# A transposed second copy of x: the first unit of a streaming encoder loads and normalises x in the layout that its projection reads

## The chip, the cores and the metric

One core of a Trainium2 chip. The metric is the device time of one execution in microseconds. The kernel was run three times, and one further execution was profiled; times of single instructions come from that profile.

## The reference

One layer of a hybrid encoder over a prompt of 2048 frames and 32 frames of a running stream, in float32. What matters here is the head of it:

```python
def rmsnorm(x, g):
    xf = x.astype(jnp.float32)
    y = xf * lax.rsqrt(jnp.mean(xf * xf, axis=-1, keepdims=True) + EPS)
    return (y * g.astype(jnp.float32)).astype(x.dtype)
...
        h = rmsnorm(yp, norm_gain[l])
        qa, ka, va, ga, qb, kb, vb, gb = split_proj(h, w_in[l])   # h @ w_in, 1024 -> 4096
        ...
        oa = band_attention_prompt(qa, ka, va, rel_bias[l])       # 8 heads x 64, own chunk and 8 before
        ob = diff_subnorm(diff_attention_prompt(qb, kb, vb, lam), subln_gain[l], lambda_init)
        yp = yp + merge_out(oa, ga, ob, gb, w_out[l])
```

A final RMS norm follows, and the new rows of the key and value caches are outputs too.

## The kernel before

The prompt is cut into 8 chunks of 256 frames (`NCH`), the 4096 columns of the input projection into 8 units of 512: units 0 to 3 are two heads of branch A each, 4 to 7 one head of branch B. The loop over `steps` takes one unit after the other (`order`), and in each unit the 8 chunks. A step projects a chunk, splits queries, keys and values, forms the softmax rows of its attention and finishes the attention of the step before.

Every float32 operand of a product is split into a high part, rounded to float32r, and a low part, the rest; a product is three matmuls (high x high, high x low, low x high). `project` (L250) takes them with the frames as the stationary operand, `project_T` (L258) with the weights; both walk over 8 k steps of 128 model columns. They need h transposed, with model columns on the partitions: tile `hT`, two parts x 8 k x 256 frames, in two buffers.

In the first unit `make_hT` (L218) builds `hT` for each chunk. `load_x` (L193) brings two tiles of 128 frames, each as two halves of 512 columns. `norm_rows` (L199) squares them on ScalarE with a sum along the row, works out one scale per frame on VectorE and ScalarE (`rstd_of`, L179) and scales the halves in place on POOL (L209). TensorE transposes them in blocks of 128x128, four to a PSUM tile (L226); ScalarE copies out the high part (L229) and VectorE subtracts for the low part (L230). SP then writes `hT` to a scratch tensor (L231), from which the later seven units load it (`load_T`). The norm's gain is folded into the weights: `load_w` (L159) loads 8 tiles of 128x512; for the first unit POOL makes gain x weight as the high part (L173) and VectorE the low part (L174).

The order of instructions on each engine is set by a planner, from the order of the program, from priorities (`ahead(n)` moves what is in it n places forward) and from a timeline that it works out; each engine then takes its instructions strictly in that order. Loads and stores are issued by SP. Tiles with tag "e" (128x512) share 16 buffers: halves of x, weights as loaded, scratch rows. PSUM tiles with tag "t" have two buffers, used by all transposes. `subnorm` (L412), in branch B, has a sum over partitions as a matmul with `onesd`, a 128x128 tile that holds 1/128 (L416).

Of the kernel before, what the change touches and what calls it, by code (L numbers as in the profile page):

```python
# [8 lines left out]
F32 = mybir.dt.float32  # L9
F32R = mybir.dt.float32r  # L10
AF = mybir.ActivationFunctionType
ALU = mybir.AluOpType
AX = mybir.AxisListType

P = 128
D = 1024
# [3 lines left out]
KT = D // P  # L20
NT = SEQ // P
NCH = NT // 2
EPS = 1e-6
LAMBDA_INIT = 0.2
NEG = -1.0e30
BAND = 640
# [4 lines left out]
def hybrid_step(  # L31
    ctx: ExitStack,
    tc: tile.TileContext,
    x_p: bass.AP,
    x_s: bass.AP,
    cak: bass.AP,
    cav: bass.AP,
# [54 lines left out]
    def e_tile(name):  # L92
        return pool.tile([P, 512], F32, name=name, tag="e", bufs=16)
# [10 lines left out]
    def t_psum():  # L104
        return psum.tile([P, 512], F32, name="t_ps", tag="t", bufs=2)
# [34 lines left out]
    def dma_here(**kw):  # L140
        tc.keep_in_program_order(SP.dma_start(**kw))
# [14 lines left out]
        ACT.activation(le, ls, AF.Exp)  # L156
        DVE.scalar_tensor_tensor(nlam, le[:, 1:2], LAMBDA_INIT, le[:, 0:1], ALU.subtract, ALU.subtract)

    def load_w(wsrc, cur_b, gain=None, tags=(("w", 10),) * KT):  # L159
        his, los = [], []  # L160
        for k in range(KT):
            raw = pool.tile([P, BAND], F32, name="wraw", tag="ea", bufs=4)[:, 0:512] if cur_b else e_tile("wraw")
            SP.dma_start(out=raw, in_=wsrc[k])
            tag, bufs = tags[k]
            w = pool.tile([P, 2, 512], F32R, name="w", tag=tag, bufs=bufs)
            hi, lo = w[:, 0, :], w[:, 1, :]
            g = 1.0 if gain is None else gain[:, k:k + 1]
            if cur_b and gain is not None and k % 2 == 0:
                ACT.activation(hi, raw, AF.Copy, scale=g)
                POOL.tensor_scalar(raw, raw, g, 0.0, ALU.mult, ALU.add)  # L170
                POOL.tensor_tensor(lo, raw, hi.bitcast(F32), ALU.subtract)  # L171
            else:
                POOL.tensor_scalar(hi, raw, g, 0.0, ALU.mult, ALU.add)  # L173
                DVE.scalar_tensor_tensor(lo, raw, g, hi.bitcast(F32), ALU.mult, ALU.subtract)  # L174
            his.append(hi)
            los.append(lo)
        return his, los
# [15 lines left out]
    def load_x(src, rows):  # L193
        xt = row_tiles("xt")
        for j in range(2):
            SP.dma_start(out=xt[j][0:rows], in_=src[:, j * 512:(j + 1) * 512])
        return xt

    def norm_rows(xt, rows):  # L199
        junk = e_tile("junk")  # L200
        ss = st_tile("ss", 2)
        for j in range(2):
            ACT.activation(junk[0:rows], xt[j][0:rows], AF.Square, accum_out=ss[0:rows, j:j + 1])
        s1 = st_tile("ss1", 1)
        DVE.tensor_tensor(s1[0:rows], ss[0:rows, 0:1], ss[0:rows, 1:2], ALU.add)
        r = rstd_of(s1, D, rows)
        for j in range(2):
            x = xt[j][0:rows]
            POOL.tensor_scalar(x, x, r[0:rows, 0:1], 0.0, ALU.mult, ALU.add)  # L209
        return xt  # L210
# [1 line left out]
    def ht_tile():  # L212
        return pool.tile([P, 2, KT, 256], F32R, name="hT", tag="hT", bufs=2)

    def load_x_chunk(c):
        return [load_x(x_pv[t * P:(t + 1) * P, :], P) for t in (2 * c, 2 * c + 1)]

    def make_hT(c, xts):  # L218
        with ahead(250):
            hT = ht_tile()  # L220
            for tt in range(2):
                h = norm_rows(xts[tt], P)
                for g in range(2):
                    tp = t_psum()
                    for j in range(4):
                        PE.transpose(out=tp[:, j * P:(j + 1) * P], in_=h[g][:, j * P:(j + 1) * P], identity=ident)  # L226
                    tv = tp.rearrange("p (k t) -> p k t", k=4)
                    ks, ts = slice(4 * g, 4 * g + 4), slice(tt * P, (tt + 1) * P)
                    ACT.copy(out=hT[:, 0, ks, ts], in_=tv)  # L229
                    DVE.tensor_tensor(hT[:, 1, ks, ts], tv, hT[:, 0, ks, ts].bitcast(F32), ALU.subtract)  # L230
            SP.dma_start(out=hT_d[c].bitcast(F32), in_=hT.bitcast(F32))  # L231
        return hT

# [422 lines left out]
        DVE.tensor_tensor(oTs[:, u, NS:2 * NS], og[:, 0:NS], oTs[:, u, 0:NS].bitcast(F32), ALU.subtract)  # L656

    ngain = const.tile([P, KT], F32, name="ngain")
    dma_here(out=ngain, in_=norm_gain)
    order = [0, 4, 5, 1, 6, 2, 7, 3]  # L660
    pend = None
    pend_s = None
# [6 lines left out]

    steps = [(n, c) for n in range(len(order)) for c in range(NCH)]  # L670

    xts = {0: load_x_chunk(0)}

    def get_hT(i):
        if i >= len(steps):
# [5 lines left out]
        return load_T(hT_d[c])  # L681

    hTn = get_hT(0)
    xts[1] = load_x_chunk(1)
    Ws = {0: load_w(w_in[order[0] // 4, order[0] % 4], False, ngain)}
    for i, (n, c) in enumerate(steps):
        u = order[n]
        isB = u >= 4
# [10 lines left out]
        QH, QL = next(qkv)  # L699
        gate = None  # L700
        if n == 0 and c + 2 < NCH:
            xts[c + 2] = load_x_chunk(c + 2)
        hTn = get_hT(i + 1)
        if n == 0 and c == 1:
            small_loads()
# [29 lines left out]
    for t in range(NT + 1):  # L735
# [31 lines left out]
            SP.dma_start(out=dst[:, cs], in_=y)  # L767


_INS = ['x_prompt', 'x_sample', 'cache_a_k', 'cache_a_v', 'cache_b_k', 'cache_b_v', 'norm_gain', 'w_in', 'w_out',  # L770
        'bias_p', 'bias_s', 'lams', 'subln', 'final_gain', 'rope_c', 'rope_s']
_OUTS = [((1, 2048, 1024), 'float32'), ((1, 32, 1024), 'float32'),
# [6 lines left out]
def _layout(inputs):  # L779
    import numpy as np  # L780
    a = {k: np.asarray(v) for k, v in inputs.items()}
    w = a['w_in'][0].reshape(KT, P, 2, 4, 4, P)
    r = {k: a[k] for k in ('x_prompt', 'x_sample', 'cache_a_k', 'cache_a_v', 'cache_b_k', 'cache_b_v', 'norm_gain')}
    r['w_in'] = w.transpose(2, 4, 0, 1, 3, 5).reshape(2, 4, KT, P, 512)
    r['w_out'] = a['w_out'][0].reshape(KT, P, 2, 512).transpose(2, 0, 1, 3)
    rb = a['rel_bias'][0]
# [40 lines left out]
```

## Time and profile before

| | us |
|---|---|
| runs | 1626.01, 1623.29, 1625.41 |
| median | 1625.41 |
| span of the profiled execution, first to last instruction | 1624.3 |
| TensorE busy in it | 1568.4 |
| VectorE busy | 1110.5 |
| ScalarE busy | 997.0 |
| POOL busy | 654.6 |

The profile gives no time of its own for the profiled execution beside its span; the span lies inside the range of the runs and 1.1 us below their median. In the rows below L12 is line 12 of the kernel. PE is TensorE's matmul, DVE is VectorE, ACT ScalarE, POOL GpSimd, SP the engine that issues the DMAs. A matmul's duration runs until its result is out, so successive matmuls overlap: what one costs is read from the distance between starts.

### The profile page before, as it was taken

To read this page: it belongs to the slowest core of one execution; us is meant where nothing else is said; L and a number is where in the kernel's file an instruction comes from. 1 tells how busy PE (TensorE), PEld (TensorE's weight loads), DVE (VectorE), ACT (ScalarE), POOL (GpSimd) and SP (SyncE) were. 2 spreads that over 40 slices of the span, in tenths; PEclk is the share of its full clock that TensorE was granted. 3 is DMA by queue.
4 is the path that set the end of the run, shared out by engine and by line. 5 is a ranking of instruction groups with operands and counts; after the bars stand their busy time and mean duration, and the time that the engine had idled before them with its cause. 6 is when DMAs were issued, how large, how long until landed. Compare 5 with 4: busy or idle time off the path is not lost.

```text
span 1624.3 us, 30799 instructions
## 1 busy us (share of the span) xinstructions
PE 1568.4 (97%) x10612; PEld 1453.1 (89%) x10612; DVE 1110.5 (68%) x3048; ACT 997.0 (61%) x2717; POOL 654.6 (40%) x1129
## 2 busy tenths in 40 slices
PE   7999999989999899999999999999999999989997
PEld 6899999978998799999998899999998999978885
DVE  5776757897588866675788856676789677743333
ACT  5776557777577766656777766565777666531111
POOL 5453434465145544353345544353446444520000
PEclk9999999999999999999999999999999999999999
DMA  7643453333332224335432153344423263334562
GB/s 275 225 172 119 176 208 131 131 122 130 125 137 86 97 102 178 122 128 195 162 136 79 66 186 124 131 148 167 159 89 129 84 240 131 131 132 161 172 210 67
DMA packets 92972, 233.92 MB, mean 144 GB/s; under 512 B 9776, under 2 KB 51888, under 8 KB 75376
## 3 DMA queue, kind: packets, MB, share of 16 engines
q1 hardware_dynamic: 92816, 231.96, 40.0%
q8 instruction: 84, 1.38, 0.3%
q14 instruction: 72, 0.59, 0.1%
HBM read 179.10 MB, written 53.74 MB: 143 GB/s over the span
## 4 chain that ended last, share of the span: by engine, by line
PE 77%; DVE 11%; ACT 5%; issue 3%; POOL 2%; DMA 1%; SPq 0%; DVEq 0%; POOLq 0%; ACTq 0%
PE z_ps L254 11%; PE z_ps L255 11%; PE z_ps L256 11%; PE t_ps L387 6%; PE z_ps L261 5%; PE z_ps L263 5%; PE z_ps L262 5%; PE s_ps L379 4%; PE s_ps L378 4%; DVE nmx L466 2%; PE o_ps L556 2%; PE o_ps L555 2%; DVE e L479 2%; DVE w L174 2%; PE o_ps L501 1%
## 5 line engine op out<-in xcount | busy, mean ns | idle before, releaser
L255 PE MATMUL z_ps<-w,hT 128*128 128x256 f32 (+2 forms) x1280 | 424.1, 332 | 4.1 <-POOL w L171 2.4
L254 PE MATMUL z_ps<-w,hT 128*128 128x256 f32 (+2 forms) x1280 | 424.7, 332 | 2.5 <-ACT hT L229 1.2
L256 PE MATMUL z_ps<-w,hT 128*128 128x256 f32 (+2 forms) x1280 | 424.1, 331 | 0.0
L255 PEld LDWEIGHTS z_ps<-w,hT 128*128 128x128 f32 x1280 | 243.5, 190 | 22.4 <-POOL w L171 3.4
L254 PEld LDWEIGHTS z_ps<-w,hT 128*128 128x128 f32 x1280 | 243.7, 190 | 19.3 <-ACT hT L229 1.7
L468 ACT ACTIVATE e<-s_ps,nmx 128x512 f32<-128x512 f32 (+3 forms) x320 | 199.1, 624 | 98.6 <-DVE nmx L466 90.5
L256 PEld LDWEIGHTS z_ps<-w,hT 128*128 128x128 f32 x1280 | 243.7, 190 | 14.1 <-issue 0.5
L397 DVE TENSOR_TENSOR pl<-t_ps,ph 128x512 fp32r<-128x512 f32 (+1 forms) x312 | 192.6, 623 | 77.8 <-ACT ph L396 75.4
L261 PE MATMUL z_ps<-hT,w 128*128 128x256 f32 x768 | 220.3, 287 | 1.7 <-DVE ql L344 1.7
L263 PE MATMUL z_ps<-hT,w 128*128 128x256 f32 x768 | 218.9, 285 | 0.0
L396 ACT CAST ph<-t_ps 128x512 fp32r<-128x512 f32 (+1 forms) x312 | 163.0, 535 | 90.5 <-PE o_ps L555 42.4
L262 PE MATMUL z_ps<-hT,w 128*128 128x256 f32 x768 | 218.4, 284 | 0.0
L378 PE MATMUL s_ps<-ks,qh 128*128 128x512 f32 (+2 forms) x544 | 194.0, 366 | 10.5 <-ACT e L468 7.8
L466 DVE TENSOR_REDUCE nmx<-s_ps 128x1 f32<-128x512 f32 (+3 forms) x320 | 187.9, 600 | 13.1 <-PE s_ps L379 9.8
L379 PE MATMUL s_ps<-ks,ql 128*128 128x512 f32 (+2 forms) x544 | 187.7, 357 | 0.1
L474 POOL TENSOR_SCALAR e<-e,da 128x512 f32<-128x512 f32 (+3 forms) x160 | 110.3, 704 | 168.5 <-DVE da L444 132.8
L261 PEld LDWEIGHTS z_ps<-hT,w 128*128 128x128 f32 x768 | 145.5, 190 | 4.9 <-PE o_ps L416 1.2
L262 PEld LDWEIGHTS z_ps<-hT,w 128*128 128x128 f32 x768 | 145.4, 189 | 2.1 <-issue 0.5
L263 PEld LDWEIGHTS z_ps<-hT,w 128*128 128x128 f32 x768 | 145.4, 189 | 1.6 <-issue 0.5
L533 POOL TENSOR_SCALAR ea<-ea,sma 128x640 f32<-128x640 f32 (+4 forms) x128 | 96.3, 754 | 115.3 <-DVE sma L532 98.7
L531 ACT ACTIVATE ea<-ea,nma 128x640 f32<-128x640 f32 (+4 forms) x128 | 97.3, 760 | 62.6 <-DVE nma L529 61.4
L378 PEld LDWEIGHTS s_ps<-ks,qh 128*128 128x128 f32 x544 | 102.2, 190 | 19.3 <-ACT e L468 12.0
(192 smaller groups left out, 3422.3 us busy)
## 6 DMA issues: line engine op xcount, KB each, us to landing
hT<-hTd SPq DMA_DIRECT2D x112, 1024.0 KB, 7.0
wraw<-in_w_in_dram SPq DMA_DIRECT2D x64, 256.0 KB, 5.0
hTd<-hT SPq DMA_DIRECT2D x8, 2048.0 KB, 7.3
oTd<-oT SPq DMA_DIRECT2D x64, 256.0 KB, 3.2
hT<-oTd SPq DMA_DIRECT2D x16, 1024.0 KB, 6.1
out_dram<-z SPq DMA_DIRECT2D x160, 64.0 KB, 1.6
xt<-in_x_prompt_dram SPq DMA_DIRECT2D x32, 256.0 KB, 5.4
y<-in_x_prompt_dram SPq DMA_DIRECT2D x32, 256.0 KB, 6.5
```

The lines of the kernel that those rows point to most:

```text
L254: PE.matmul(zp, hT[:, 0, k, ts], his[k][:, cols], start=(k == 0), stop=False)
L255: PE.matmul(zp, hT[:, 0, k, ts], los[k][:, cols], start=False, stop=False)
L256: PE.matmul(zp, hT[:, 1, k, ts], his[k][:, cols], start=False, stop=(k == KT - 1))
L261: PE.matmul(zp, his[k][:, cols], hT[:, 0, k, :], start=(k == 0), stop=False)
L262: PE.matmul(zp, his[k][:, cols], hT[:, 1, k, :], start=False, stop=False)
L263: PE.matmul(zp, los[k][:, cols], hT[:, 0, k, :], start=False, stop=(k == KT - 1))
L378: PE.matmul(sp[:, 0:w], QH[:, m, qs], ks[:, m, kc], start=True, stop=False)
L379: PE.matmul(sp[:, 0:w], QL[:, m, qs], ks[:, m, kc], start=False, stop=True)
L396: ACT.copy(out=hv, in_=tv)
L397: DVE.tensor_tensor(lv, tv, hv.bitcast(F32), ALU.subtract)
L466: DVE.tensor_reduce(nmx[:, m, b:b + 1], sp[:, 0:w], AX.X, ALU.max, negate=True)
L468: ACT.activation(e[:, 0:w], sp[:, 0:w], AF.Exp, bias=nmx[:, m, b:b + 1], accum_out=sm[:, m, b:b + 1])
```

## The change

The host lays x out a second time, `x_t`, as chunk x 128 partitions x 8 k x 256 frames. `load_xT` loads a chunk of it as four tiles of 128 x (2 k x 256 frames), 256 KB each as before. `scales_T` squares them on ScalarE, adds the four tiles and the two k of the rest to one 128x256 tile (VectorE for the first chunk, POOL for the others), and sums it over the partitions with one matmul with `onesd`, which leaves the sum on all partitions; the scale per frame is then worked out as a whole 128x256 tile `rb`. `make_hT` multiplies each tile by `rb` on VectorE, copies the high part on ScalarE and subtracts for the low part on POOL. There are no transposes of the prompt's x left on TensorE. The 32 frames of the running stream are treated as before, and the last stage still reads x row by row.

The weights of the first unit are loaded ahead of the second chunk's x, four of the eight tiles in buffers of another tag ("ea"); their high parts are made on ScalarE and POOL in turn, their low parts on VectorE. The load of the gain, the first chunk's loads and these weights get priorities further forward.

```diff
-    def load_w(wsrc, cur_b, gain=None, tags=(("w", 10),) * KT):
+    def raw_w(wsrc, k, ea):
+        raw = pool.tile([P, BAND], F32, name="wraw", tag="ea", bufs=4)[:, 0:512] if ea else e_tile("wraw")
+        SP.dma_start(out=raw, in_=wsrc[k])
+        return raw
+
+    def load_w(wsrc, cur_b, gain=None, tags=(("w", 10),) * KT, raws=None):
...
+            if raws is not None:
+                if k % 2:
+                    ACT.activation(hi, raw, AF.Copy, scale=g)
+                else:
+                    POOL.tensor_scalar(hi, raw, g, 0.0, ALU.mult, ALU.add)
+                DVE.scalar_tensor_tensor(lo, raw, g, hi.bitcast(F32), ALU.mult, ALU.subtract)
+            elif cur_b and gain is not None and k % 2 == 0:
...
-    def load_x_chunk(c):
-        return [load_x(x_pv[t * P:(t + 1) * P, :], P) for t in (2 * c, 2 * c + 1)]
-
-    def make_hT(c, xts):
+    def load_xT(c, js=range(4)):
+        xs = [e_tile("xT").rearrange("p (k t) -> p k t", k=2) for _ in js]
+        for x, j in zip(xs, js):
+            SP.dma_start(out=x, in_=x_t[c, :, 2 * j:2 * j + 2, :])
+        return xs
+
+    def scales_T(xs, add):
+        sq = [e_tile("sqT").rearrange("p (k t) -> p k t", k=2) for _ in xs]
+        for a, x in zip(sq, xs):
+            ACT.activation(a, x, AF.Square)
+        add(sq[0], sq[0], sq[1], ALU.add)
+        add(sq[2], sq[2], sq[3], ALU.add)
+        add(sq[0], sq[0], sq[2], ALU.add)
+        sm = sq[0][:, 0, :]
+        add(sm, sm, sq[0][:, 1, :], ALU.add)
+        ps = t_psum()[:, 0:256]
+        PE.matmul(ps, onesd, sm, start=True, stop=True)
+        v = pool.tile([P, 256], F32, name="vT", tag="sq", bufs=1)
+        DVE.tensor_scalar(v, ps, P / D, EPS, ALU.mult, ALU.add)
+        r = pool.tile([P, 256], F32, name="rT", tag="rs", bufs=1)
+        ACT.activation(r, v, AF.Ln)
+        ACT.activation(r, r, AF.Exp, scale=-0.5)
+        rb = pool.tile([P, 256], F32, name="rb", tag="rb", bufs=1)
+        DVE.tensor_tensor(rb, r, r, ALU.mult)
+        DVE.tensor_tensor(rb, rb, v, ALU.mult)
+        DVE.tensor_scalar(rb, rb, -0.5, 1.5, ALU.mult, ALU.add)
+        DVE.tensor_tensor(rb, rb, r, ALU.mult)
+        return rb
+
+    def make_hT(c, xs):
         with ahead(250):
             hT = ht_tile()
-            for tt in range(2):
-                h = norm_rows(xts[tt], P)
-                for g in range(2):
-                    tp = t_psum()
-                    for j in range(4):
-                        PE.transpose(out=tp[:, j * P:(j + 1) * P], in_=h[g][:, j * P:(j + 1) * P], identity=ident)
-                    tv = tp.rearrange("p (k t) -> p k t", k=4)
-                    ks, ts = slice(4 * g, 4 * g + 4), slice(tt * P, (tt + 1) * P)
-                    ACT.copy(out=hT[:, 0, ks, ts], in_=tv)
-                    DVE.tensor_tensor(hT[:, 1, ks, ts], tv, hT[:, 0, ks, ts].bitcast(F32), ALU.subtract)
+            rb = scales_T(xs, DVE.tensor_tensor if c == 0 else POOL.tensor_tensor)
+            for j, x in enumerate(xs):
+                ks = slice(2 * j, 2 * j + 2)
+                DVE.tensor_tensor(x, x, rb.unsqueeze(1).broadcast_to([P, 2, 256]), ALU.mult)
+                ACT.copy(out=hT[:, 0, ks, :], in_=x)
+                POOL.tensor_tensor(hT[:, 1, ks, :], x, hT[:, 0, ks, :].bitcast(F32), ALU.subtract)
             SP.dma_start(out=hT_d[c].bitcast(F32), in_=hT.bitcast(F32))
         return hT
...
-    dma_here(out=ngain, in_=norm_gain)
+    with ahead(1100):
+        SP.dma_start(out=ngain, in_=norm_gain)
...
-    xts = {0: load_x_chunk(0)}
+    wsrc = w_in[order[0] // 4, order[0] % 4]
+    with ahead(1000):
+        xts = {0: load_xT(0)}
+        raws = [raw_w(wsrc, k, k < 4) for k in range(KT)]
...
     hTn = get_hT(0)
-    xts[1] = load_x_chunk(1)
-    Ws = {0: load_w(w_in[order[0] // 4, order[0] % 4], False, ngain)}
+    with ahead(200):
+        Ws = {0: load_w(wsrc, True, ngain, raws=raws)}
+    xts[1] = load_xT(1)
...
-            xts[c + 2] = load_x_chunk(c + 2)
+            xts[c + 2] = load_xT(c + 2)
...
+    r['x_t'] = a['x_prompt'][0].reshape(NCH, 256, KT, P).transpose(0, 3, 2, 1)
```

## Rows read from the trace of the kernel before

**Rows 1.** The page: busy time of each engine, and its chain by engine.

```profile
PE 1568.4 (97%) x10612; PEld 1453.1 (89%) x10612; DVE 1110.5 (68%) x3048; ACT 997.0 (61%) x2717; POOL 654.6 (40%) x1129
...
PE 77%; DVE 11%; ACT 5%; issue 3%; POOL 2%; DMA 1%; SPq 0%; DVEq 0%; POOLq 0%; ACTq 0%
```

**Rows 2.** Stretches, chunks 1-4: us, busy PE PEld DVE ACT POOL, clock, DMA, GB/s.

```profile
30.30:45.40 15.10, 15.10 (x128) 15.02 (x127) 8.03 (x29) 9.28 (x27) 2.93 (x7) 1.00 0.33 140
45.40:64.80 19.40, 16.90 (x135) 15.93 (x133) 13.00 (x51) 16.55 (x53) 7.00 (x12) 1.00 0.78 279
64.80:85.00 20.20, 19.89 (x154) 19.63 (x155) 16.70 (x53) 15.06 (x43) 10.56 (x21) 0.92 0.50 184
85.00:108.60 23.60, 22.13 (x177) 21.02 (x177) 19.92 (x68) 19.47 (x61) 15.58 (x29) 1.00 0.43 151
```

**Rows 3.** Timeline of TensorE at a group of transposes: start, us, instruction, count.

```profile
80.87 0.28 PE L262 MATMUL z_ps<-hT,w 128*128 128x256 f32 x1
80.99 0.60 PE L226 MATMUL t_ps<-ident,xt 128*128 128x128 f32 x4
81.34 0.36 PE L556 MATMUL o_ps<-pl,vt 128*128 128x256 f32 x1
81.55 0.28 PE L555 MATMUL o_ps<-ph,vt 128*128 128x256 f32 x1
```

**Rows 4.** Timeline of TensorE at a column sum (L416) of the second unit.

```profile
245.31 0.59 PE L416 MATMUL o_ps<-sq,onesd 128*128 128x256 f32 x2
245.55 0.47 PE L261 MATMUL z_ps<-hT,w 128*128 128x256 f32 x1
245.85 0.28 PE L262 MATMUL z_ps<-hT,w 128*128 128x256 f32 x1
```

**Rows 5.** Timeline of TensorE ahead of chunk 3; idle before, releaser in brackets.

```profile
62.61 1.33 PE L226 MATMUL t_ps<-ident,xt 128*128 128x128 f32 x8 [1.66 <-POOL xt L209]
...
64.76 0.39 PE L254 MATMUL z_ps<-w,hT 128*128 128x256 f32 x1 [0.83 <-ACT hT L229]
```

**Rows 6.** Groups by shape, POOL: count | busy us, mean ns | idle before.

```profile
L477 POOL TENSOR_TENSOR e<-e 128x512 f32<-128x512 f32 x40 | 58.1, 1454 | 0.3
...
L171 POOL TENSOR_TENSOR w<-wraw,w 128x512 fp32r<-128x512 f32 x16 | 22.3, 1402 | 0.1
L209 POOL TENSOR_SCALAR xt<-xt,rr 128x512 f32<-128x512 f32 x32 | 21.9, 697 | 11.7 <-ACT rr L185 5.9 <-DVE rr L190 2.4 <-DMA xt<-in_x_prompt_dram 2.3
```

**Rows 7.** The same of VectorE, then one of ScalarE.

```profile
L479 DVE SCALAR_TENSOR_TENSOR e<-e,da 128x512 f32<-128x512 f32 x72 | 74.1, 1034 | 14.6 <-POOL e L474 14.3
...
L766 DVE SCALAR_TENSOR_TENSOR y<-y,rr,fg 128x512 f32<-128x512 f32 x32 | 23.0, 760 | 0.6
...
L230 DVE TENSOR_TENSOR hT<-t_ps,hT 128x512 fp32r<-128x512 f32 x32 | 21.7, 687 | 9.5 <-ACT hT L229 9.3
...
L421 DVE SCALAR_TENSOR_TENSOR on<-o_ps,gcol,rs 128x256 f32<-128x256 f32 x32 | 15.1, 471 | 5.2 <-ACT rs L419 5.1
...
L419 ACT ACTIVATE rs<-rs 128x256 f32<-128x256 f32 x32 | 13.4, 418 | 0.4
```

**Rows 8.** By stretch, POOL's row scalings (L209) alone, chunks 2 to 4.

```profile
45.40:64.80 19.40, 2.29 (x4) 1.00 0.78 279
64.80:85.00 20.20, 5.99 (x9) 0.92 0.50 184
85.00:108.60 23.60, 6.80 (x10) 1.00 0.43 151
```

**Rows 9.** Timeline of the start: ScalarE, TensorE, VectorE, and POOL last.

```profile
7.52 0.63 ACT L203 ACTIVATE junk<-xt 128x512 f32<-128x512 f32 x1 [0.46 <-DMA xt<-in_x_prompt_dram]
...
13.27 0.56 PE L254 MATMUL z_ps<-w,hT 128*128 128x256 f32 x1
...
20.68 0.74 DVE L174 SCALAR_TENSOR_TENSOR w<-wraw,ngain,w 128x512 fp32r<-128x512 f32 x1
...
12.04 8.11 POOL L173 TENSOR_SCALAR w<-wraw,ngain 128x512 fp32r<-128x512 f32 x8 [0.17 <-DMA wraw<-in_w_in_dram]
```

More of the change, by code (lines that the diff above doesn't have):

```diff
@@ L34, in hybrid_step @@
     x_p: bass.AP,
+    x_t: bass.AP,
     x_s: bass.AP,
@@ L157, in small_loads @@
         DVE.scalar_tensor_tensor(nlam, le[:, 1:2], LAMBDA_INIT, le[:, 0:1], ALU.subtract, ALU.subtract)
-    def load_w(wsrc, cur_b, gain=None, tags=(("w", 10),) * KT):
+    def raw_w(wsrc, k, ea):
[3 more added lines that the diff above has]
+    def load_w(wsrc, cur_b, gain=None, tags=(("w", 10),) * KT, raws=None):
         his, los = [], []
         for k in range(KT):
-            raw = pool.tile([P, BAND], F32, name="wraw", tag="ea", bufs=4)[:, 0:512] if cur_b else e_tile("wraw")
-            SP.dma_start(out=raw, in_=wsrc[k])
+            raw = raw_w(wsrc, k, cur_b) if raws is None else raws[k]
             tag, bufs = tags[k]
@@ L167, in load_w @@
             g = 1.0 if gain is None else gain[:, k:k + 1]
-            if cur_b and gain is not None and k % 2 == 0:
+            if raws is not None:
[5 more added lines that the diff above has]
+            elif cur_b and gain is not None and k % 2 == 0:
                 ACT.activation(hi, raw, AF.Copy, scale=g)
@@ L767, in hybrid_step @@
             SP.dma_start(out=dst[:, cs], in_=y)
-_INS = ['x_prompt', 'x_sample', 'cache_a_k', 'cache_a_v', 'cache_b_k', 'cache_b_v', 'norm_gain', 'w_in', 'w_out',
+_INS = ['x_prompt', 'x_t', 'x_sample', 'cache_a_k', 'cache_a_v', 'cache_b_k', 'cache_b_v', 'norm_gain', 'w_in', 'w_out',
         'bias_p', 'bias_s', 'lams', 'subln', 'final_gain', 'rope_c', 'rope_s']
```

## The prediction

> **What bounds the kernel now.** I read the page's busy times first, then the chain that ended last: TensorE is busy for 97% of the span and carries 77% of the chain [rows 1]. The reader is to see there that time comes off this kernel only where TensorE gets less to do or waits less. The change works in the first unit alone, so I cut that unit into its chunks with busy times by stretch (each stretch starts with the first projection matmul of a chunk): in chunks 1 to 4 TensorE is busy for all but a little, and POOL for 3 to 16 of the 15 to 24 us [rows 2]. Then the timeline of TensorE, for what a transpose and a float32 column sum cost between other matmuls [rows 3, 4] and where TensorE stands idle [rows 5]. Last the groups of instructions, for the price of what the other engines gain and lose [rows 6, 7], and the start [rows 9].
>
> **TensorE.** *Removed:* 16 transposes a chunk, in groups of four. One group starts at 80.99, and the next matmul at 81.34; that matmul is followed after 0.21 us, where the one ahead of the group was followed after 0.12 [rows 3]. So a group costs 0.35 + 0.09 = 0.44 us of TensorE and a chunk 4 x 0.44 = 1.76 us. *Added:* one column sum a chunk, a float32 product of onesd with 256 columns. The trace has it elsewhere: L416 writes the same shape, as two instructions. It starts at 245.31, the second matmul after it at 245.85; less the 0.12 us of the one between, it costs 0.54 - 0.12 = 0.42 us [rows 4]. Net 1.76 - 0.42 = 1.34 us a chunk, and over chunks 1 to 7, where TensorE is full, 7 x 1.34 = **9.4 us** less. Chunk 0 is in the start, below.
>
> **The one stall of TensorE in this unit.** Ahead of chunk 3 TensorE waits 1.66 us for POOL's normalised rows and 0.83 us for ScalarE's copy [rows 5], and in the stretch after it the granted clock is 0.92 on average, that is 1.2 GHz for a part of it and 2.4 GHz for the rest; 20.2 us x 0.08 = 1.6 us of work lost [rows 2]. The waited-for instructions (row scale, transposes, copy out of PSUM) all go. What is late next is the column sum and the low parts, costed below as pacing; the old stall itself I count as gone: 2.5 + 1.6 = **4.1 us** less. Its bounds are 0 (the new chain stalls at the same place) and 4.1.
>
> **POOL, and what it can take back.** *Removed:* four row scalings of 0.70 us a chunk [rows 6]. *Added*, from chunk 1 on: three sums of 128x512 and one of 128x256, and the four low parts of 128x512, all two-input operations out of SBUF. The same form is there twice: 1.45 us (L477) and 1.40 us (L171) [rows 6]. Seven at 1.43 and one at half of that make 10.7 us a chunk in place of 2.8. Beside it stands POOL's other work, the stretch's busy time less the row scalings: 2.9 at most in chunk 1, 7.0 - 2.3 = 4.7 in chunk 2, 10.6 - 6.0 = 4.6 in chunk 3, 15.6 - 6.8 = 8.8 in chunk 4 [rows 2, 8]. So POOL comes to 13.6, 15.4, 15.3 and 19.5 us, while TensorE, less the 1.34 us and the stall, would need 15.1 - 1.3 = 13.8, 19.4 - 2.5 - 1.3 = 15.6, 20.2 - 1.6 - 1.3 = 17.3 and 23.6 - 1.3 = 22.3 us. In chunks 1 and 2 the two engines are even; in chunk 3 there are 2 us of room, in chunk 4 nearly 3. The row scalings were done ahead in bunches (nine and more in the stretches of chunks 3 and 4 [rows 8], four to a chunk); the new sums can go ahead as well, but the low parts can't: they wait for one of the two hT buffers. TensorE's projection takes one low part for two of its eight k steps, so a POOL that comes late holds the projection there. For the three builds that fall into the start and chunks 1 and 2 I take 1.5 us each, **4.5 us** more, about one two-input operation late per build. The bounds are 0 and the full path: sums 5.0 + low parts 5.7 = 10.7 us against the 2.8 of today, nearly 8 us a build.
>
> The trace shows VectorE's form with two SBUF inputs at 1.03 us where POOL is busy and at 0.76 where it is idle, so a busy POOL costs it 0.27 us an operation [rows 7]. The Trainium skill ("SBUF — State Buffer", Who interferes with whom) goes further: the port pair that VectorE and GPSIMD share is an exclusive lock, so a VectorE operation with two SBUF inputs and a GPSIMD operation that reads SBUF would never run together. By the rows I have the pacing above; by that rule it would be the first rival below.
>
> **VectorE and ScalarE.** *VectorE:* four low parts of 0.69 us out of PSUM go [rows 7], with ten one-column operations that I leave out on the safe side. In come four products of 128x512 with rb, both inputs in SBUF: the bounds for that form are 0.76 us with POOL idle (L766) and 1.03 us with POOL busy (L479), and I take the upper one since POOL will be busy [rows 7]; and five of 128x256 at no more than 0.47 (L421) [rows 7]. That is 4.1 + 2.4 - 2.8 = 3.7 us a chunk more, on an engine busy for 8.0 of 15.1 and 19.9 of 23.6 us in the stretches [rows 2]; it stays just under TensorE, so it costs nothing by itself, but if its cover goes in chunk 4 (19.9 + 3.7 = 23.6 against 22.3 us for TensorE) it costs 1.3 us. *ScalarE:* squares and copies stay four each; a logarithm and an exponential of 0.42 us [rows 7] come in for reads of accumulators and one-column functions: even.
>
> **The chain of one build** is longer. From the last square today: statistics, row scale, transposes, copy: the last square of chunk 0 starts at 7.52 and the first projection matmul runs at 13.3. New: sums, column sum, five operations and two functions of 0.42 to 0.47, product, copy. VectorE makes the sums in chunk 0, and of them only two follow the last square (0.8 and 0.5 us), so 8.2 + 1.3 + 0.9 (the column sum at half clock) + 7 x 0.45 + 1.0 + 0.6 = about 15.1: 1.8 us later. **Start:** against that, W's eight loads go ahead of the second chunk's x. Today POOL makes eight high parts from 12.04 to 20.15 and VectorE's last low part ends at 21.42 [rows 9], which paces TensorE. Then four high parts go to ScalarE, and POOL is free for them. VectorE has 8 low parts, 3.5 sums and 4 products at 0.9, the middle of L766 and L479, and 2.4 us of scales [rows 7]: 16.4 us. From the last square's start without a pause it ends at 23.9, less what it did before, against 21.4. I take **0** for the start: the earlier W against the later x; bounds -1.5 and +2.5. The queue of SP: the norm gain stays first, x of chunk 0 next, W past x of chunk 1 (four issues); the second chunk is due at 30, more than 10 us behind its landing either way.
>
> **The sum.** -9.4 - 4.1 + 4.5 + 0 = -9.0 us. The profiled execution's span is 1624.3 us; the median of the runs is 1625.4, 1.1 us above it, which I take as it is. 1624.3 - 9.0 + 1.1 = **1616.4 us**. With the bounds of the terms short of the full pacing the forecast's own range is 1610 to 1622. All later units are as full of TensorE as this one [rows 1], so what comes off here has no other engine to be given back to; but the order of later instructions is planned anew, and I allow 2 us to either side for that.
>
> **Rivals.** *VectorE and POOL get in each other's way, no change.* If the two couldn't read SBUF at the same time at all, the chunk would need their sum: for chunks 1 to 3 13.6, 15.4 and 15.3 on POOL plus 4 x 0.76 + 3 x 0.47 = 4.4 on VectorE, 18.0, 19.8 and 19.7 us against 13.8, 15.6 and 17.3: 4.2 + 4.2 + 2.4 = 10.8 us back, and with some 2 us in chunk 4 12.8 of the gain of 9.4 + 4.1 = 13.5 is gone: 1624.7. Against it: at the start POOL's eight and VectorE's eight weight operations, 8 x 0.70 (POOL's one-input price at L209) + 8 x 0.76 = 11.7 us alone, are done between 12.04 and 21.42, in 9.4 us [rows 6, 7, 9]: they overlap in part. So the trace shows slowing, but no full exclusion.
>
> *The column sum stands in TensorE's queue, slower.* TensorE takes its instructions in order. The column sum waits for POOL's last sum; behind it in the queue stand the attention matmuls of the chunk before and then the projection. If POOL makes the 5.0 us of sums behind its softmax scalings instead of ahead, TensorE stands for them in each of seven builds. It decides once a build loses more than the 1.34 us that it gains. At half of the sums exposed, 2.5 us a build, and 1.3 us of lost clock with it (today's one stall of 2.5 us cost 1.6), it is 7 x 3.8 = 26.6 us more against 13.5 less: 1638.5. For it: POOL goes to 99% of TensorE's time in chunks 1 and 2, and its queue has waits of its own. Against: 16 buffers of this size let x and its squares be loaded and summed a chunk ahead.
>
> **Chances.** Forecast (1610 to 1622): 0.55. No change: 0.2, some of it still just faster. Slower by the column sum: 0.25. A measurement of this kernel tells 0.2%, 3.3 us, from no change. Faster 0.58, same 0.17, slower 0.25. The range 1607 to 1635 takes in the forecast, the case without change and the lower half of the slower one.
>
> **What would show it.** Right: no transposes at the old place and groups of two column-sum instructions instead; TensorE without a wait in chunks 1 to 3, projection matmuls at their 0.12 us pitch; the first matmul of the second unit about 9 us earlier. Wrong: waits of the column sum for POOL, or of the third projection matmul of a k step for the low part; POOL over 95% busy in chunks 1 to 4; a granted clock below 0.95 in those stretches; VectorE's products with rb well above 1.03 us; a start that ends more than 2 us later.

## The result, and the profile after

| | before | after |
|---|---|---|
| median of 4 runs side by side, us | 1624.56 | 1652.25 |
| range, us | 1623.29 to 1626.01 | 1650.87 to 1653.94 |
| span of the profiled execution, us | 1624.3 | 1652.1 |

The changed kernel takes 1.0172 times as long (95% interval 1.0158 to 1.0185): 27.7 us slower, where 9 us faster was forecast. First the page of after, busy times and the chain by engine, against [rows 1]:

```profile
PE 1563.4 (95%) x10500; PEld 1444.5 (87%) x10500; DVE 1130.6 (68%) x3012; ACT 1004.2 (61%) x2673; POOL 711.8 (43%) x1153
...
PE 72%; DVE 12%; ACT 6%; issue 4%; POOL 3%; DMA 2%; SPq 1%; DVEq 0%; POOLq 0%; ACTq 0%
```

TensorE has less to do, as intended, and is busy for a smaller share. The first unit, from its first projection to that of the second unit, in a row for each kernel (stretch, us; busy PE, PEld, DVE, ACT, POOL; granted clock, DMA share, GB/s). Before:

```profile
13.30:175.90 162.60, 156.54 (x1231) 150.25 (x1230) 117.25 (x369) 113.32 (x314) 73.67 (x140) 0.99 0.51 191
```

After, and then chunks 1 to 4 as in [rows 2]:

```profile
26.00:206.20 180.20, 161.05 (x1141) 151.54 (x1142) 127.17 (x327) 115.55 (x274) 123.89 (x162) 0.93 0.43 156
...
45.04:62.70 17.66, 16.33 (x116) 15.51 (x116) 10.64 (x34) 10.54 (x28) 8.72 (x12) 0.90 0.28 119
62.70:89.98 27.28, 21.97 (x157) 19.38 (x157) 21.37 (x67) 20.94 (x52) 20.26 (x29) 1.00 0.64 209
89.98:111.03 21.05, 17.38 (x115) 16.54 (x115) 12.77 (x23) 12.52 (x26) 17.11 (x17) 0.83 0.47 167
111.03:135.03 24.00, 22.66 (x168) 21.93 (x167) 17.06 (x52) 17.66 (x46) 15.28 (x24) 0.93 0.28 111
```

The account: the unit starts 26.0 - 13.3 = 12.7 us later and lasts 180.2 - 162.6 = 17.6 us longer; of these 30.3 us, 2.5 come back in the later units. Inside the unit TensorE is idle for 19.1 instead of 6.1 us (13.0 more), and the clock costs 0.07 x 180.2 = 12.6 instead of 1.6 us (11.0 more): TensorE falls to 1.2 GHz (granted clock 0.50) at 46.0, 90.4, 110.9, 138.2 and 162.1 us, each time within 1.6 us behind a wait of 1.2 to 3.2 us; three waits of 1.0 to 1.3 us (62.1, 80.5 and 135.0) were not followed by it. TensorE's work, busy time less what the clock cost, goes from 156.5 - 1.6 = 154.9 to 161.1 - 12.6 = 148.5 us: 6.4 us less, where the forecast had 9.4. The three make 13.0 + 11.0 - 6.4 = 17.6 us. TensorE's waits up to the second unit (who waited for whom: total us, times, longest):

```profile
PE t_ps L242 <- DVE sqT L240: 18.3, 1, 18.3
PE z_ps L287 <- ACT hT L262: 10.9, 4, 6.5
PE s_ps L412 <- DVE ql L376: 6.6, 3, 2.9
PE s_ps L411 <- DVE mxa L559: 2.6, 2, 2.4
PE z_ps L289 <- POOL hT L263: 1.7, 3, 0.8
```

The column sum (L242) waits in the start. The projection waits for ScalarE's copy of the products, hardly for POOL's low parts; attention waits for the low parts of q, which stand behind four products in VectorE's queue. The start on VectorE (start, us, instruction; in brackets idle before and releaser), against [rows 9]:

```profile
9.94 0.75 DVE L178 SCALAR_TENSOR_TENSOR w<-wraw,ngain,w 128x512 fp32r<-128x512 f32 x1 [8.92 <-DMA wraw<-in_w_in_dram]
10.61 0.68 DVE L236 TENSOR_TENSOR sqT<-sqT 128x512 f32<-128x512 f32 x1
...
17.84 0.41 DVE L240 TENSOR_TENSOR sqT<-sqT 128x256 f32<-128x256 f32 x1
...
22.31 1.24 DVE L251 TENSOR_SCALAR rb<-rb 128x256 f32<-128x256 f32 x1
23.58 0.90 DVE L252 TENSOR_TENSOR rb<-rb,rT 128x256 f32<-128x256 f32 x1
24.51 1.90 DVE L261 TENSOR_TENSOR xT<-xT,rb 128x512 f32<-128x512 f32 x3
```

A low part of W stands ahead of the first sum and waits for its DMA. And the groups by shape, against [rows 4, 6, 7] (count | busy us, mean ns | idle before):

```profile
L263 POOL TENSOR_TENSOR hT<-xT,hT 128x512 fp32r<-128x512 f32 x32 | 46.4, 1477 | 16.5 <-ACT hT L262 16.4
L261 DVE TENSOR_TENSOR xT<-xT,rb 128x512 f32<-128x512 f32 x32 | 30.0, 1000 | 0.1
...
L242 PE MATMUL t_ps<-sqT,onesd 128*128 128x256 f32 x16 | 5.5, 427 | 18.4 <-DVE sqT L240 18.3
...
L251 DVE TENSOR_SCALAR rb<-rb 128x256 f32<-128x256 f32 x8 | 4.2, 527 | 0.1
```

### The profile page after: what moved, and what is told of

Same layout as the page of the kernel before. It is cut to its first block, busy times and chain, and to the rows that moved or that the text cites. A ratio compares the mean times of both kernels' runs of the same rounds, so it can differ in the third digit from the quotient of the medians.

```text
span 1652.1 us, 30483 instructions
## 1 busy us (share of the span) xinstructions
PE 1563.4 (95%) x10500; PEld 1444.5 (87%) x10500; DVE 1130.6 (68%) x3012; ACT 1004.2 (61%) x2673; POOL 711.8 (43%) x1153
## 4 chain that ended last, share of the span: by engine, by line
PE 72%; DVE 12%; ACT 6%; issue 4%; POOL 3%; DMA 2%; SPq 1%; DVEq 0%; POOLq 0%; ACTq 0%
PE z_ps L287 11%; PE z_ps L288 11%; PE z_ps L289 11%; PE t_ps L420 6%; PE s_ps L412 4%; PE s_ps L411 4%; PE z_ps L294 4%; PE z_ps L296 4%; PE z_ps L295 4%; DVE nmx L499 2%; PE o_ps L589 2%; PE o_ps L588 2%; DVE e L512 2%; ACT e L501 2%; PE o_ps L534 1%
## 5 line engine op out<-in xcount | busy, mean ns | idle before, releaser
L287 PEld LDWEIGHTS z_ps<-w,hT 128*128 128x128 f32 x1280 | 247.9, 194 | 33.7 <-issue 8.8
L288 PEld LDWEIGHTS z_ps<-w,hT 128*128 128x128 f32 x1280 | 247.8, 194 | 20.3 <-DVE w L185 4.8
L289 PEld LDWEIGHTS z_ps<-w,hT 128*128 128x128 f32 x1280 | 246.8, 193 | 15.8 <-POOL hT L263 2.6
L411 PE MATMUL s_ps<-ks,qh 128*128 128x512 f32 (+2 forms) x544 | 193.6, 367 | 14.0 <-ACT e L501 10.8
L499 DVE TENSOR_REDUCE nmx<-s_ps 128x1 f32<-128x512 f32 (+3 forms) x320 | 188.5, 601 | 13.6 <-PE s_ps L412 9.8
```

What stands on the lines that cost most here:

```text
L287: PE.matmul(zp, hT[:, 0, k, ts], his[k][:, cols], start=(k == 0), stop=False)
L288: PE.matmul(zp, hT[:, 0, k, ts], los[k][:, cols], start=False, stop=False)
L289: PE.matmul(zp, hT[:, 1, k, ts], his[k][:, cols], start=False, stop=(k == KT - 1))
L411: PE.matmul(sp[:, 0:w], QH[:, m, qs], ks[:, m, kc], start=True, stop=False)
L499: DVE.tensor_reduce(nmx[:, m, b:b + 1], sp[:, 0:w], AX.X, ALU.max, negate=True)
```

## The experiments

Each time stands against the kernel before on the same chip; "against before" is the ratio with its 95% interval. Theory O: order on VectorE and the longer chain. P: POOL's operations pace the unit. L: the latency from column sum to projection. S: the small loads. C: POOL's two-input operations hold up VectorE's.

The later units differ between the profiled executions, too, though no variant changes what they do: from the second unit on 1448.4 us before, 1445.9 after, 1436 to 1447 in the variants. The planner orders their instructions anew each time, and single executions of one kernel differ (those of the kernel before, over all chips, from 1620.4 to 1629.8). What a variant does to the first unit is therefore read from the start of its second one as well: 175.9 us before, 206.2 after.

**e1_wlow_behind.** W's low parts of the first chunk pinned behind each product.

```diff
+                if mid:
+                    mid(j)      # two low parts of W
```

> The changed kernel with one thing moved: in the first chunk VectorE's eight low parts of W stand behind the sums, the scales and the products (two after each product), instead of ahead of and between the sums. Theory O (order: in the start VectorE waits in its own queue for the weights' DMAs while the squares of x lie ready): the column sum moves from 18.3 to about 11 us, the first projection from 26.0 to 16 to 18 us, and the whole kernel comes 6 to 11 us earlier: about 1643 against 1652. Theory P (POOL's two-input sums and low parts pace the whole first unit): the start is earlier, but chunk 1 then waits for POOL's sums and low parts; the first projections of chunks 2 and 3 stay at about 62.7 and 90.0 us, and the time stays within 3 us of 1652.

1655.04 us, against before 1.0180 (1.0159 to 1.0201), no gain. The column sum moved to 9.85 and the first projection to 17.55, but chunk 1 began at 44.72 us as in the changed kernel (45.04). Theory O's cause of the late start is real, but the time doesn't go by it: the next build is late anyway. Its timeline shows why. VectorE:

```profile
16.06 0.69 DVE L268 TENSOR_TENSOR xT<-xT,rb 128x512 f32<-128x512 f32 x1
...
18.00 1.75 DVE L268 TENSOR_TENSOR xT<-xT,rb 128x512 f32<-128x512 f32 x1
...
21.00 1.76 DVE L268 TENSOR_TENSOR xT<-xT,rb 128x512 f32<-128x512 f32 x1
```

POOL, at the same time:

```profile
17.69 1.51 POOL L272 TENSOR_TENSOR hT<-xT,hT 128x512 fp32r<-128x512 f32 x1
20.49 1.73 POOL L272 TENSOR_TENSOR hT<-xT,hT 128x512 fp32r<-128x512 f32 x1 [1.29 <-ACT hT L271]
```

The product takes 0.69 us when POOL is idle, and 1.75 when it begins some 0.3 to 0.5 us behind a two-input operation of POOL: it ends 0.5 us after that one.

**e2_sums_dve, e4_lows_dve, e5_all_dve.** Sums, low parts, or both to VectorE.

```diff
-            rb = scales_T(xs, DVE.tensor_tensor if c == 0 else POOL.tensor_tensor)
+            rb = scales_T(xs, DVE.tensor_tensor)
-                POOL.tensor_tensor(hT[:, 1, ks, :], x, ...)
+                DVE.tensor_tensor(hT[:, 1, ks, :], x, ...)
```

> The changed kernel with the sums of squares of chunks 1 to 7 on VectorE instead of POOL (POOL keeps the low parts of h). Theory P (POOL's sums and low parts pace the unit): about 5 us a chunk come off the pace of POOL, 10 us or more come back: 1642 or less. Theory O (the chain on VectorE and its order): POOL was not late; VectorE gets 3.5 us a chunk more at its end of the queue: 1648 to 1656, no better than 4 us.

> The changed kernel with the four low parts of h of each chunk on VectorE instead of POOL (POOL keeps the sums). Theory P: POOL's 5.7 us a chunk come off its pace: 5 us or more come back, 1647 or less. Theory O: the low parts were hardly waited for (1.7 us in the whole unit), and VectorE, in whose queue the products, the scales and the low parts of q stand, gets 3 to 4 us a chunk more: 1652 to 1664.

> The changed kernel with both the sums of squares and the low parts of h on VectorE in every chunk; POOL has no part in the build. Theory P (POOL's operations with two inputs, and what they do to VectorE's): with no such operation of POOL left in the build, VectorE's products and sums take 0.69 us each throughout, and the gains seen with the sums alone (6.5 us) and the low parts alone (12.7 us) add up: 1630 to 1636. Theory O (VectorE's own queue is what is late): 4 x 0.69 us of low parts and 3.5 x 0.69 us of sums a chunk more stand in it, and what the low parts gave is partly given back: 1640 to 1650.

Sums: 1645.79, against before 1.0125 (1.0110 to 1.0140). Low parts: 1639.51, 1.0087 (1.0069 to 1.0105). Both: 1644.72, 1.0114 (1.0092 to 1.0135). Taking the low parts from POOL gives 12.7 us although TensorE had waited 1.7 us for them, which was against theory O; and the two don't add, against theory P. But most of the 12.7 us doesn't come where the low parts are made. The first unit of e4:

```profile
25.80:202.97 177.17, 158.05 (x1143) 147.24 (x1144) 136.21 (x368) 116.78 (x278) 80.22 (x131) 0.95 0.44 158
```

Its second unit starts at 203.0, 3.2 us earlier than after; the other 8.1 of the 11.3 us between the two profiled executions come in later units.

**e3_no_stats.** No squares, sums, column sum and scales.

```diff
-            rb = scales_T(xs, ...)
+            rb = ones_rb
```

> The changed kernel without squares, sums, column sum and scales: the products take a tile of ones, so the normalisation of x is left out. This prices the whole chain from x to the scales in all eight builds. Theory O: the product needs only x, so the waits of TensorE for ScalarE's copies in chunks 0 to 7 (some 11 us) and most of the half clock behind them go: 20 to 30 us less than the changed kernel, 1622 to 1632. Theory P: the sums are gone from POOL but the low parts stay on it: 8 to 15 us less, 1637 to 1644.

1601.06, against before 0.9852 (0.9834 to 0.9871): both theories too small. The first unit:

```profile
11.09:160.50 149.41, 144.11 (x1126) 138.98 (x1127) 114.08 (x300) 94.38 (x235) 98.97 (x139) 1.00 0.57 213
```

It lasts 149.4 us against 162.6 before, 13.2 less: 1.6 of the clock, 0.8 of idle time and 10.8 of TensorE's work, where the forecast's price for seven chunks of transposes is 7 x 1.76 = 12.3. So that price was about right. The statistics cost 51 us in all; at the start of the second unit (160.5 against 206.2) it is 45.7.

**e6_scales_early.** Scales of the next chunk ahead of the projection.

```diff
+        if n == 0 and c + 1 < NCH:
+            scales(c + 1)
         qkv = chunk_qkv(u, isB, c, hTn, W, kss, vts)
```

> The changed kernel with squares, sums, column sum and scales of the next chunk put into the program ahead of the projection of the chunk before, so that the column sum stands earlier in TensorE's queue; all engines do the same work. Theory L (the 9 to 12 us from column sum to first projection are late because the column sum stands behind the previous chunk's projection in TensorE's queue): the column sums of chunks 1 to 7 move ahead by 5 to 15 us, the waits for ScalarE's copies go, 5 to 12 us less: 1640 to 1647. Theory P: the low parts and the sums still take POOL and VectorE the same time: within 3 us of 1652.

1659.01, against before 1.0203 (1.0182 to 1.0225), slower. The column sum of chunk 1 came at 21.84 instead of 35.37, but its scale operations now fell beside POOL's low parts, and ScalarE's copies of the projection, which the transposes of k need, stood behind its copies of h (waits of 4.5 and 2.8 us). VectorE:

```profile
30.16 1.21 DVE L249 TENSOR_TENSOR rb<-rT 128x256 f32<-128x256 f32 x1 [1.12 <-ACT rT L247]
31.40 1.38 DVE L250 TENSOR_TENSOR rb<-rb,vT 128x256 f32<-128x256 f32 x1
32.82 1.27 DVE L251 TENSOR_SCALAR rb<-rb 128x256 f32<-128x256 f32 x1
34.12 1.40 DVE L252 TENSOR_TENSOR rb<-rb,rT 128x256 f32<-128x256 f32 x1
```

Operations of 0.42 us (0.29 for L251) take 1.21 to 1.40, one for each operation of POOL.

**e7_small_late, e10_small_early.** The small loads in chunk 4, or right behind W.

```diff
-        if n == 0 and c == 1:
+        if n == 0 and c == 4:      # e10: DMAs ahead of the loop, their work at c == 1
             small_loads()
```

> The changed kernel with the small loads (rope tables, lambda) issued in chunk 4 of the first unit instead of chunk 1, so that they don't stand in SyncE's queue behind the store of h of chunk 2 with VectorE waiting for them. Theory S (that queue costs the 27.3 us between the first projections of chunks 2 and 3, against 19.4 in the kernel before): this stretch falls to 20 to 22 us and 4 to 7 us come off the whole: 1645 to 1648. If the stretch is long for another reason, it stays above 25 us and the time stays within 3 us of 1652.

> The changed kernel with the small loads (rope tables, lambda) issued right behind the loads of W and of the second chunk, ahead of every store of h; their small VectorE and ScalarE work stays in chunk 1's place in the program. Theory S (the small loads stood behind the store of h of chunk 2 and held VectorE and ScalarE in order; issued in chunk 4 they held the sample rows instead): the first projections of chunks 2 and 3 come within 19 to 21 us of each other instead of 27.3, nothing takes the place, and 6 to 9 us come off: 1643 to 1646. If the lateness of the builds takes the time back elsewhere, as after the issue in chunk 4: 1649 or more.

In the changed kernel they stood behind the store of h, and loads of x behind them. SyncE's queue, then VectorE's:

```profile
65.32 0.32 SPq L264 DMA_DIRECT2D hTd<-hT  x1
...
68.47 1.21 SPq L142 DMA_DIRECT2D lt<-in_lams_dram  x1
69.78 5.83 SPq L229 DMA_DIRECT2D xT<-in_x_t_dram  x8
```

```profile
75.24 0.40 DVE L153 TENSOR_TENSOR lt<-lt 128x128 f32<-128x128 f32 x1 [0.18 <-DMA lt<-in_lams_dram]
75.67 0.42 DVE L376 SCALAR_TENSOR_TENSOR ql<-z_ps,qh 64x256 fp32r<-64x256 f32 x1
```

Late: 1651.58, against before 1.0161 (1.0138 to 1.0184); the stretch of chunk 2 fell from 27.3 to 17.8 us, but then the sample rows' loads stood behind them and TensorE waited 10.8 us for those. Early: 1648.47, 1.0149 (1.0132 to 1.0166); the stretch is 16.8 us, yet only 3.8 us come off the whole, the later chunks being longer. Theory S holds for the place, at half the price. Its mechanism isn't shown: VectorE stood for the last small load for 0.18 us only, the loads of x went out some 4 us later for them, and the early issue changes the planner's order, too.

**e9_combo_w, e11_rows_first, e12_best.** e11: first chunk as before. e12: that, small loads early, low parts on VectorE. e9: the repairs e1, e2, e4, e6 and e7 together, but for chunk 1's scales, which keep their place.

```diff
-            hT = make_hT(c, xts.pop(c))
+            hT = (make_hT if c else make_hT_rows)(c, xts.pop(c))
```

> All that is suspected taken back at once on the changed kernel: sums and low parts of h on VectorE, the scales of the next chunk ahead of the projection, small loads in chunk 4, and in the first chunk W's low parts behind the products. If late builds are the whole of the loss, TensorE keeps the 9.4 us that the transposes leave, the start is 4 us later than before at most, and the time is 1612 to 1624, no longer than that of the kernel before. If VectorE with some 14 us of build a chunk becomes the bound, it stays above 1632.

> The changed kernel with the first chunk as in the kernel before (x by rows, row scale, transposes on TensorE, W loaded behind the second chunk's x and split as before); chunks 1 to 7 in the new layout. Theory O (the longer chain and the weights cost the start 12.7 us): the first projection comes back to about 13.3 and 9 to 13 us come off: 1639 to 1643. Theory P (what is saved in the start is waited for in chunk 1, as when only W's low parts were moved): the first projection of chunk 1 is no earlier than 42 us, and the time stays above 1648.

> Three parts together: the first chunk as in the kernel before, the small loads early, and the low parts of h in chunks 1 to 7 on VectorE (sums stay on POOL). If the three causes are separate, their gains add (about 11, 8 and 10 us): 1620 to 1626, even with the kernel before or a little faster. If they are one and the same lateness, the sum is no better than the best of them: 1635 or more.

e9 1639.42, against before 1.0085 (1.0066 to 1.0105); e11 1649.69, 1.0151 (1.0136 to 1.0167); e12 1639.83, 1.0092 (1.0077 to 1.0107). With the old first chunk the first projection is at 14.25, but chunk 1 begins at 37.73 instead of 30.3 [rows 2]; in e9 9.1 us are once more a wait for the sample rows. TensorE in e11:

```profile
30.16 0.59 PE L261 MATMUL t_ps<-sqT,onesd 128*128 128x256 f32 x2
...
37.73 0.58 PE L306 MATMUL z_ps<-w,hT 128*128 128x256 f32 x1 [3.34 <-ACT hT L281]
```

From the column sum to the projection are 7.6 us, and chunk 0's attention has too little for TensorE in between: it is busy for 3.5 us of them. The causes overlap: their gains don't add.

**e13_before_small_early.** The kernel before with e10's edit.

> The kernel before with nothing but the small loads issued early, right behind the loads of W. It tells whether the stall ahead of chunk 3 of the kernel before (2.5 us of waits and 1.6 us of clock) was the same queue. If it was: 2 to 5 us less, 1620 to 1623, and the first projection of chunk 3 without a wait. If it was POOL's row scaling as such: within 2 us of the kernel before.

1622.25, against before 0.9978 (0.9969 to 0.9988), 2.9 us faster than the runs beside it, the best of all variants that normalise x. Chunk 3 begins at 62.17 without a wait, instead of 64.76 [rows 5]: issuing the small loads early takes the old stall away, with POOL's row scaling as it was. How they made it isn't shown: VectorE doesn't stand for them in the kernel before. And the stall isn't worth the forecast's 4.1 us, for chunk 4 gives most of it back (27.5 us, where [rows 2] has 23.6):

```profile
81.91:109.37 27.46, 25.36 (x181) 23.49 (x180) 23.25 (x76) 21.83 (x67) 16.86 (x31) 0.89 0.41 140
```

The second unit starts at 175.5 instead of 175.9; the rest of the 2.9 us comes later.

**e14_no_dep, e15_no_newton.** Products by a constant tile, the scales computed all the same; and the scales without their refinement.

```diff
-                DVE.tensor_tensor(x, x, rb..., ALU.mult)
+                DVE.tensor_tensor(x4, x4, onesd..., ALU.mult)      # e14
-        DVE.tensor_tensor(rb, r, r, ALU.mult)                      # e15: these four
...
+        return r
```

> The changed kernel with the whole chain of squares, sums, column sum and scales computed as it stands, but the products multiply by a tile of constants instead of the scales: the normalisation of x is left out, the work is not. Theory L (latency: the build waits for the scales, 9 to 12 us after the column sum, with nothing else for TensorE): the waits for ScalarE's copies of h go and the time comes close to the kernel without statistics (1601) plus 3 us of column sums and some crowding: 1604 to 1615. Theory O (occupation and order of VectorE and POOL): the operations are all still there, 1640 or more.

> The changed kernel without the four VectorE operations behind the exponential (the refinement of the scales is left out). The chain from column sum to product is shorter by the four operations and by what stands between them on VectorE, some 3 to 4 us of 9 to 12. Theory L: 7 builds and the start, 2 to 4 us each: 16 to 30 us less, 1622 to 1636. Theory O: 1.6 us a chunk of VectorE work less that TensorE doesn't wait for: 1645 to 1652.

e14: 1634.48, against before 1.0062 (1.0043 to 1.0080): 18 us come from the products' dependency, and 33 of the 51 stay with operations whose results nobody uses; neither theory's number. TensorE waits for those even so: for column sums, and for the PSUM tile of one that VectorE has yet to read:

```profile
PE t_ps L421 <- DVE vT L244: 4.0, 1, 4.0
```

e15: 1636.81, 1.0077 (1.0051 to 1.0102), 15.4 us less, 0.8 us above the range of L: 1.9 us for each of eight builds, about what the four operations take (18 us in all on VectorE). Its second unit starts at 192.6, so 13.6 us are gained by then.

**e16_lows_twice.** e4, and POOL makes the low parts again for nobody.

```diff
                 DVE.tensor_tensor(hT[:, 1, ks, :], x, hT[:, 0, ks, :].bitcast(F32), ALU.subtract)
+                POOL.tensor_tensor(sq[j], x, hT[:, 0, ks, :].bitcast(F32), ALU.subtract)
```

> The kernel with the low parts of h on VectorE (1639.5), and POOL makes the same four low parts a chunk a second time, into tiles that nobody reads: POOL is as busy as in the changed kernel, but the projection doesn't wait for it. Theory C (POOL's two-input operations hold up VectorE's): the 12.7 us come back, 1648 to 1655, and VectorE's products and scales beside them take 1.2 to 1.8 us again. If what cost was the wait for POOL's own low parts: 1638 to 1643.

1679.29, against before 1.0333 (1.0305 to 1.0362): 39.8 us above e4, three times what C asked for. (POOL's other work stands behind the copies too, and the tiles of the squares are held longer, so this isn't C alone.) POOL, then VectorE:

```profile
23.39 6.60 POOL L264 TENSOR_TENSOR sqT<-xT,hT 128x512 f32<-128x512 f32 x4 [5.58 <-ACT hT L262]
```

```profile
23.72 1.76 DVE L261 TENSOR_TENSOR xT<-xT,rb 128x512 f32<-128x512 f32 x1
25.40 6.82 DVE L263 TENSOR_TENSOR hT<-xT,hT 128x512 fp32r<-128x512 f32 x4
```

One operation of each in 1.7 us, again and again.

**e18_rb_psum.** The scales in PSUM, nothing else.

```diff
-        rb = pool.tile([P, 256], F32, name="rb", tag="rb", bufs=1)
+        rb = tp[:, 256:512]      # tp: the column sum's PSUM tile
```

> The changed kernel with the scales of x kept in the free half of the column sum's PSUM tile instead of in SBUF, so that three of the four scale operations and all 32 products have one operand in PSUM; work, order of the program and engines stay. Theory C (POOL's two-input operations hold up those of VectorE that take all operands out of SBUF): products and scale operations keep 0.7 and 0.42 us beside POOL's sums and low parts (in the changed kernel they take up to 1.78 and 1.51 us), the builds come earlier, 4 to 12 us less: 1640 to 1648. If an operand in SBUF is enough to be held up: the products still go up to 1.7 us and the time stays at 1650 to 1656, or above it since a PSUM tile is held for longer.

1639.67, against before 1.0093 (1.0071 to 1.0115): 12.6 us less. Groups by shape:

```profile
L264 POOL TENSOR_TENSOR hT<-xT,hT 128x512 fp32r<-128x512 f32 x32 | 40.6, 1302 | 20.4 <-ACT hT L263 20.4
...
L262 DVE TENSOR_TENSOR xT<-xT,t_ps 128x512 f32<-128x512 f32 x32 | 19.8, 680 | 0.1
```

The products go from 1000 to 680 ns on average, the longest from 1777 to 689, and POOL's low parts from 1477 to 1302. Theory C holds: one operand's place settles whether they are held up. What that is worth is less sure. The first unit:

```profile
23.79:198.65 174.86, 160.84 (x1145) 151.00 (x1146) 117.66 (x335) 116.28 (x277) 117.28 (x164) 0.93 0.45 162
```

2.2 us come in the start and 5.3 in the first unit; the other 5.0 come in later units, where these operations don't run.

**e17_rows_to_3, e19_rows_to_1.** The old layout up to chunk 3 (e17, low parts on VectorE) or chunk 1 (e19, scales in PSUM), the new one behind; small loads early.

> Chunks 0 to 3 as in the kernel before (rows, row scale, transposes), chunks 4 to 7 in the new layout with the low parts on VectorE, small loads early. The comparison is with the kernel before with small loads early (1622.3). Theory L: in chunks 4 to 7 TensorE has 8 us and more of attention to cover the chain, so the 1.34 us of each of four chunks appear: 1614 to 1620. If VectorE's order makes the builds late there too: 1622 to 1632.

> Chunks 0 and 1 as in the kernel before (rows, transposes), chunks 2 to 7 in the new layout with the scales in PSUM (sums and low parts on POOL), small loads early. To be compared with the kernel before with small loads early (1622.3). If the three causes are the whole loss, TensorE keeps 6 x 1.34 = 8 us: 1614 to 1618. If the rest of the chain (column sum, four scale operations, products ahead of the low parts of q in VectorE's queue) still makes builds late: 1622 to 1630.

e17 1626.02, against before 1.0004 (0.9990 to 1.0019); e19 1624.38, 1.0001 (0.9991 to 1.0012); e13, with the same small loads, stands at 0.9978. So even there the transposes' gain isn't seen in the time. From chunk 3 to the second unit, e13 and then e19:

```profile
62.17:175.49 113.32, 110.54 (x865) 105.77 (x863) 80.82 (x252) 76.69 (x202) 48.62 (x101) 0.97 0.43 158
```

```profile
63.27:181.91 118.64, 110.38 (x806) 104.27 (x807) 88.42 (x246) 80.94 (x193) 78.64 (x121) 0.93 0.41 151
```

TensorE is idle for 8.3 instead of 2.8 us, and the clock takes 0.07 x 118.6 = 8.3 instead of 0.03 x 113.3 = 3.4 us: 10.4 us more together. Its work falls by 5.0 us (107.1 to 102.1), close to the forecast's 4 x 1.34 = 5.4 for the builds of chunks 4 to 7. Which of the short waits a better order would take away wasn't tried.

## Why the prediction was wrong

- *9.4 us of TensorE: held in part.* The transposes' price was about right (10.8 of 12.3 us in e3), but in the changed kernel TensorE's work fell by 6.4 us; what makes up the rest isn't shown. Of the column sums of chunks 1 to 7 only chunk 3's waits for POOL's sums, for 0.4 us, so the second rival, too, wasn't what happened.
- *The old stall as gone (4.1 us): wrong.* The prediction took the named releaser, POOL's row scaling, for the cause. The stall goes with the row scaling in place once the small loads are issued early (e13), and is worth 0.4 us by the second unit. In the changed kernel the same stretch, of chunk 2, went from 19.4 [rows 2] to 27.3 us, and to 16.8 with the small loads early (e10).
- *POOL's pacing (4.5 us): the wrong mechanism.* TensorE waited 1.7 us for low parts.
- *"It costs nothing by itself" (VectorE, 3.7 us a chunk): the failed step.* The price of a product was right, 1.03 taken and 1.00 measured, but by luck: 21 of the 32 took 0.69 us and eight 1.75 to 1.78. And products and scales were set against VectorE's throughput only; the chain of a build was followed in the start alone. They stand in the chain of every next build and ahead of the low parts of q, and TensorE waited 13.0 us more. Leaving four short ones out gave 15.4 us (e15), 13.6 of them by the second unit; holding fewer up gave 12.6 (e18), 7.6 of them by the second unit.
- *The first rival (VectorE and POOL exclude each other) was put aside by a misread row.* That its price, 12.8 us, is e18's 12.6 is luck: the rival added up engine times of chunks 1 to 4, and 5.0 of the 12.6 us come in later units. Against it stood that the weight operations of the start took 9.4 us and not 11.7 [rows 6, 7, 9]: 0.80 of the sum. But e16's pair takes 1.70 us and not 0.68 + 1.30 = 1.98, which is 0.86 of the sum, and that is the full effect: operations alternate one for one, and only their ends overlap. The start of the kernel before had shown the lock, VectorE and then POOL:

```profile
13.15 2.98 DVE L174 SCALAR_TENSOR_TENSOR w<-wraw,ngain,w 128x512 fp32r<-128x512 f32 x3
16.05 0.68 DVE L230 TENSOR_TENSOR hT<-t_ps,hT 128x512 fp32r<-128x512 f32 x1
...
13.37 5.60 POOL L173 TENSOR_SCALAR w<-wraw,ngain 128x512 fp32r<-128x512 f32 x5
```

Side by side VectorE's operations take 1.0 us and not 0.74, POOL's 1.1 and not 0.70; VectorE's one with an operand in PSUM (L230) keeps 0.68. The Trainium skill ("SBUF — State Buffer", Who interferes with whom) says that a VectorE instruction with two SBUF inputs contends with a GpSimd instruction that reads SBUF, and that one with at most one SBUF input outside the two-port modes does not. e18 agrees (689 ns at most); that the loser blocks fully agrees but for the overlapped ends. L251 has one SBUF input and is held up all the same (0.29 to 1.27 us in e6); whether it runs in such a mode no run shows.
- *The start at 0 (-1.5 to +2.5): 12.7.* The sums were taken to run first on VectorE; in its queue W's low parts stood ahead. Yet undoing this gave 0 (e1) to 2.6 us (e11): "the second chunk is due at 30" counted its landing, not its build, and no variant with statistics in the new layout began chunk 1 before 37.7.
- *The clock of new waits was not in the forecast's sum.* 11.0 us of the loss are TensorE at 1.2 GHz behind waits of 1.2 to 3.2 us.
- *2 us for the order of later instructions: too little.* They became 2.5 us shorter here, and up to 12 in the variants, single executions' differences included.

Open: the gains overlap, so the 27.7 us can't be split among the causes; and e14 leaves 33 us with operations whose results nobody uses. Of these only C's part was tried (e18), and how much the waits for column sums and their PSUM tiles make isn't known.

## What to carry to other kernels

Taking work off the bounding engine pays only if what replaces it is ready in time: follow the new chain from its data to the first matmul that needs it, in the first chunks above all, and count a short wait with the clock behind it. Put operands of VectorE beside a busy POOL into PSUM where that is possible. When a wait names an engine, that engine may be late for another reason: move what stands ahead of it, measure again, and look where in the run the time changes.

## What the runs showed of the hardware

A VectorE operation out of SBUF alone that began during a two-input operation of POOL ended about 0.55 us (128x512) or 0.28 us (128x256; 0.15 for L251) behind POOL's end. So 0.69 became up to 1.76 us (e1), 0.42 up to 1.40, and 0.29 became 1.27 (e6); POOL's went from 1.30 to 1.65 where the two alternate (e16). With one operand in PSUM the same operation kept 0.68 us, and POOL's took 1.30 (e18).
